# Merged instruction streams in a hybrid diffusion step: a recorder that counts changes between whole and part-array products

## The chip, the cores and the metric

The kernel runs on one core of a Trainium2 chip. The metric is the device time of one execution in microseconds; lower is better. The engines of the core work side by side, each through its own instructions in the order in which the program was written: TensorE (PE in the profile, its weight loads PEld), VectorE (DVE), ScalarE (ACT), GpSimd (POOL), and SyncE (SP), which issues the DMAs. They wait for each other by semaphores.

## The reference

One step of a two-layer backbone in f32. There are 128 prompt tokens and 1024 sample tokens, 1152 together, of width 1024. Each layer does the following (cut to what matters):

```python
h = rms_norm(x, g) * (1 + scale) + shift          # scale, shift, gate from the condition
parts = split_columns(h @ w_in)                   # one projection, 8384 columns
o_a = mla_attention(...) * silu(gate_a)           # latent attention, 8 heads, 1152 keys
o_b = b_in * short_conv(c_in * x_in, w) * silu(gate_b)
o_c = gdn_branch(...)                             # gated DeltaNet, both directions
m = s_a * (o_a @ w_pa) + s_b * (o_b @ w_pb) + s_c * (o_c @ w_pc)   # s_* = sigmoid(merge_g)
x = x + gate * (m @ w_o)
```

The DeltaNet works in chunks of 64 tokens with 8 heads of 64 x 64. In every chunk a triangular system is solved, and the chunks of a head are chained by their state:

```python
def step(state, xs):
    u_i, w_i, qd_i, kd_i, at_i, gl_i = xs
    v_new = u_i - einsum('bhck,bhkv->bhcv', w_i, state)
    o_i = einsum('bhck,bhkv->bhcv', qd_i, state) + einsum('bhij,bhjv->bhiv', at_i, v_new)
    state = state * exp(gl_i)[..., None, None] + einsum('bhck,bhcv->bhkv', kd_i, v_new)
    return state, o_i
```

## The kernel before

**Stages.** `start` loads and computes the modulation and the first normalised tokens. Then each layer goes through `front` (line 795: projection, convolutions, DeltaNet, and then the expansion of the latents), `attention` (written out by hand, without the recorder) and `mix` (line 1955: gates, branch projections, output projection, the next layer's norm, and the first tiles of the next layer's projection).

**Whole products.** The token axis is cut in three pieces of 384. Activations and weights of the projections are split into a high and a low part of f32r, and one tile of 128 x 128 weights makes three products of 128 rows, 128 columns and 384 tokens: `ip` in the projection (8 row blocks, so 24 products for a tile and a piece of tokens; 38 column tiles in `front`, four more in the attention), `mg`, `pp`, `wop` in `mix`, `ukp`, `uvp`, `uqp` for the latents. They use the whole array.

**Part-array products.** The DeltaNet's products are f32 and small, and each uses a part of the array, so that several can lie beside each other. An f32 product shows as two matmuls in the trace. `s_ga` (line 1540) makes the decay (`sg`, a whole product) and the chunk products `G` (64 x 64, 128 columns), `s_gb` solves the 32 x 32 triangles on VectorE and GpSimd without TensorE, `s_gz` (line 1715) joins them with 16 products of 32 x 32 (`pw`) from `P`, ScalarE's copy `ws`, and 16 more, then four copies by ScalarE. `s_gc` (line 1762) is the recurrence: for each of 16 steps and each of four pairs of heads, four products `p` (state by key), a scaling on VectorE and two adds of `vT` into the two halves of `scr`, four products `pv` whose inputs are these halves, a scaling, four products `pk`, and two updates of the state `SH` on VectorE, one for each direction. A fifth job does the prompt in two steps, four chunks at once. `s_gd` (line 1868) makes the outputs: `oi` (query by state) and `oa`. The four or more products of one phase alternate the direction, so that the second product needs the second half of what VectorE makes.

**The order of the work.** All of this is written as generators ("streams"). While one runs, `Eng` (line 82) does not issue an instruction but records it as an `Op` with its engine, what it reads and writes, and a cost in us (`cost`, line 115). `Flow.run` (line 228) merges the streams: it looks at the first open instruction of each, works out when it could start by its own clock (`ready`, line 159, from costs and a table of lags between engines; and `free`, when the engine is done), takes the best, and `put` (line 189) advances the clock and issues the instruction for good. So the order on every engine is fixed when the program is built, by the costs that the recorder believes. The choice weighs the time with a rank:

```python
best = min(cand, key=lambda x: (x[0] + 0.02 * x[1], x[1]))
...
    WIN = 0.3
    PREF = 0.5
...
RK = dict(ad=1, mk=0, mkb=5, xl=0, adl=1, w=2, ip=9, ev=1, cv=4, la=0, ga=7, gb=6, gv=4, gz=4, gc=3, gd=4, w2=2, lb=3, ln=0, ln1=1,
```

A smaller rank goes first. The projection `ip` has rank 9, the last of all: it fills the time in which the DeltaNet's streams (`ga` to `gd`, ranks 3 to 7) are not ready. A stream of better rank that will be ready a little later than the chosen one is waited for (`WIN`, `PREF`). `front` first runs the merged streams until the DeltaNet is done, and then goes on with what is left of `ip` beside the latents' streams (`lb`, `ln`).

**The prices before.** An f32r product costs `n / 2400` us from 256 columns on, an f32 one `4 n / 2400`. A product with at most 64 weight rows costs its weight columns over 1200 (over 600 where its output begins at partition 0). A change between whole and part-array products costs nothing.

Of the kernel before, what the change touches and what calls it, by code (L numbers as in the profile page):

```python
# [39 lines left out]


class Op:
    __slots__ = ("e", "f", "r", "w", "c", "m")


class Wait:
# [35 lines left out]
class Eng:  # L82
# [7 lines left out]
    def __getattr__(self, m):  # L90
        real = getattr(self.real, m)

        def call(*a, **kw):
            if not self.k.rec:
                return real(*a, **kw)  # L95
            op = Op()
            op.e = self.e
            op.f = lambda: real(*a, **kw)  # L98
            aps = [x for x in a if hasattr(x, "tensor")]
            out = kw.get("out")  # L100
            outs = [out] if out is not None else [aps.pop(0)]
            if kw.get("accum_out") is not None:
                outs.append(kw["accum_out"])
            ins = aps + [v for n, v in kw.items() if n not in ("out", "accum_out") and hasattr(v, "tensor")]
            if m == "matmul" and not kw.get("start", True):
                ins.append(outs[0])
            op.w = [(self.k.key(x), _span(x)) for x in outs]
            op.r = [(self.k.key(x), _span(x)) for x in ins]
            op.c = self.cost(m, outs[0], ins, kw)
            op.m = ins[0].ap[-1][1] / 1200.0 if self.e == "PE" else 0.0  # L110
            return op

        return call

    def cost(self, m, out, ins, kw):
        n = max([_free(out)] + [_free(x) for x in ins if x.space != DRAM]) if self.e != "PE" else _free(out)
        if self.e == "PE":
            if m == "transpose":
                return n * 2 / 2400.0
            r = ins[1].dtype == F32R  # L120
            t = n * ((1 if n >= 256 else 4) if r else 4) / 2400.0
            if ins[0].ap[0][1] <= 64:
                t = ins[0].ap[-1][1] / (1200.0 if out.offset // out.ap[0][0] else 600.0)
            return t
# [9 lines left out]
        for x in [out] + ins:  # L134
            c = 1
# [8 lines left out]
class Flow:  # L144
# [8 lines left out]
    def __init__(self, k):  # L153
        self.k = k
        self.free = {}
        self.log = {}
        self.ev = set()

    def ready(self, op):
        t = 0.0  # L160
# [28 lines left out]
    def put(self, op, s):  # L189
        f = self.free  # L190
        if op.e == "SP":
            f["SP"] = s + 0.06
            hw = max(s, f.get("HW", 0.0))
            f["HW"] = hw + 0.45
            d = max(hw + 1.1, f.get("DMA", 0.0))
            f["DMA"] = d + op.c
            self.note(op, d + op.c)
        else:
            if op.e == "PE":
                s = max(s, f.get("PEW", 0.0) + op.m)  # L200
                f["PEW"] = s
            f[op.e] = s + op.c
            self.note(op, s + op.c)
        op.f()
# [23 lines left out]
    def run(self, streams, until=None, evs=()):  # L228
# [5 lines left out]
        while True:  # L234
# [8 lines left out]
            cand = []  # L243
            for n in names:
                op = streams[n]["head"]
                if op is not None:
                    cand.append((max(self.free.get(op.e, 0.0), self.ready(op)), streams[n]["rank"], n, op))
            if not cand:
                raise RuntimeError("streams wait for each other: %s" % {n: streams[n]["wait"] for n in names})
            best = min(cand, key=lambda x: (x[0] + 0.02 * x[1], x[1]))  # L250
            for x in cand:
                if x[3].e == best[3].e and x[1] < best[1]:
                    wait = x[0] - best[0]
                    if wait <= 0 or wait < self.WIN and wait < self.PREF * (best[3].c - wait):
                        best = x
                        break
            streams[best[2]]["head"] = None
            self.put(best[3], best[0])

    WIN = 0.3  # L260
    PREF = 0.5


RK = dict(ad=1, mk=0, mkb=5, xl=0, adl=1, w=2, ip=9, ev=1, cv=4, la=0, ga=7, gb=6, gv=4, gz=4, gc=3, gd=4, w2=2, lb=3, ln=0, ln1=1,
# [2053 lines left out]
```

## Time and profile before

| | |
|---|---|
| median of 3 runs | 3682.22 us (3678.1 to 3687.41) |
| the profiled execution | 3702.81 us, its span 3701.0 us |
| PE busy | 3543.0 us (96%), 24330 matmuls |
| PEld busy | 3080.1 us (83%) |
| DVE busy | 1969.5 us (53%) |
| POOL busy | 1396.8 us (38%) |
| ACT busy | 1102.2 us (30%) |
| DMA | 336.79 MB, 91 GB/s over the span |
| mean granted TensorE clock | 0.957 of full speed |
| largest matmul groups | `ip` x5328, 1167.0 us, mean 358 ns; `mg` x3456, 623.2 us, mean 335 ns; `pp` x1728, 329.2 us, mean 341 ns |

The span runs from the first to the last instruction. Matmuls are pipelined: a single one is shown with its whole passage through the array, so that the shown duration (358 ns) is longer than the distance to the next one. Distances between the starts of rows in the timeline tell more than durations. In the timeline equal neighbours are merged into one row with their number; an idle time before a row stands in brackets with what ended it.

### The profile page before, as it was taken

Reading aid. Unit: us, or ns where it says so; the run is one execution under the profiler, and the core shown is the slowest. Engines: PE = TensorE matmul, PEld = TensorE weight load, DVE = VectorE, ACT = ScalarE, POOL = GpSimd, SP = SyncE. Lnnn points to the kernel's source line nnn. Section 1 sums busy time; section 2 is a strip of 40 time slices with the busy share of each in tenths; the row PEclk is TensorE's granted clock in tenths of the full one; section 3 lists DMA queues with packets and bytes.
Section 4 is the critical chain, followed back from the end, with each engine's and each line's share of the span. In section 5 each row is a group of like instructions: output and inputs, shape, how many; then the busy total and the mean of one; then the engine's idle time right before and its main releaser. Section 6 shows DMA issues by size and latency. Waiting matters only on the chain. (4 is left out here: it accounts for less than half of the span.)

```text
span 3701.0 us, 62464 instructions
## 1 busy us (share of the span) xinstructions
PE 3543.0 (96%) x24330; PEld 3080.1 (83%) x24330; DVE 1969.5 (53%) x4492; ACT 1102.2 (30%) x2327; POOL 1396.8 (38%) x1456
## 2 busy tenths in 40 slices
PE   7999999998999999999999999999999999999998
PEld 4988777777876789999999877777887667999998
DVE  4477676755555234541575777776455542131236
ACT  4432222224233222221344232212242332121234
POOL 3165555432266401332122645653323662123311
PEclk8999899999998899999999989999999998999999
DMA  5332212225622133441233222311364222132222
GB/s 184 93 106 74 57 54 72 68 59 171 185 66 67 47 111 113 121 127 52 101 101 95 87 75 79 77 48 55 98 223 117 69 61 67 56 95 61 81 79 88
DMA packets 315207, 336.79 MB, mean 91 GB/s; under 512 B 146208, under 2 KB 231904, under 8 KB 314528
## 3 DMA queue, kind: packets, MB, share of 16 engines
q1 hardware_dynamic: 314912, 332.80, 30.6%
q8 instruction: 192, 3.15, 0.3%
q14 instruction: 103, 0.84, 0.1%
HBM read 240.16 MB, written 92.47 MB: 90 GB/s over the span
## 5 line engine op out<-in xcount | busy, mean ns | idle before, releaser
L98 PE MATMUL ip<-h,wh_wi 128*128 128x384 f32 x5328 | 1167.0, 358 | 2.3 <-DVE gb L98 1.1
L98 PEld LDWEIGHTS ip<-h,wh_wi 128*128 128x128 f32 x5328 | 933.0, 194 | 54.4 <-issue 15.9
L98 PE MATMUL mg<-h,wh_mg 128*128 128x384 f32 x3456 | 623.2, 335 | 2.5 <-ACT mt L98 2.5
L98 PEld LDWEIGHTS mg<-h,wh_mg 128*128 128x128 f32 x3456 | 602.0, 188 | 3.1 <-ACT mt L98 3.1
L95 POOL TENSOR_TENSOR acc<-acc,P 128x512 f32<-128x512 f32 x224 | 290.2, 1295 | 199.7 <-ACT P L95 188.0
L95 DVE TENSOR_REDUCE mx<-s 128x1 f32<-128x384 f32 (+1 forms) x400 | 206.8, 540 | 240.4 <-PE s L95 239.3
L98 PE MATMUL pp<-ob,wp 128*128 128x384 f32 x1728 | 329.2, 341 | 2.3 <-DVE mU L98 1.2
L98 POOL TENSOR_TENSOR tmp<-M,X 128x2 f32<-128x2 f32 (+30 forms) x310 | 217.7, 702 | 277.1 <-DVE X L98 258.2
L98 PEld LDWEIGHTS pp<-ob,wp 128*128 128x128 f32 x1728 | 305.9, 191 | 11.1 <-DVE mt L98 6.6
L95 PE MATMUL st<-q,K 97*128 97x512 f32 (+1 forms) x912 | 290.4, 434 | 0.0
L95 ACT ACTIVATE P<-st 128x512 f32<-128x512 f32 x292 | 174.5, 598 | 351.4 <-PE st L95 314.7
L98 POOL TENSOR_TENSOR wh_mg<-wrm,wh_mg 128x512 fp32r<-128x512 f32 x88 | 117.1, 1333 | 424.0 <-ACT wh_mg L98 353.5
L98 POOL TENSOR_TENSOR mU<-mU,mt 128x384 f32<-128x384 f32 x96 | 108.3, 1128 | 327.2 <-DVE mt L98 327.1
L95 PEld LDWEIGHTS st<-q,K 97*128 97x128 f32 x912 | 185.1, 215 | 42.7 <-issue 24.3
L98 POOL TENSOR_TENSOR wh_wi<-wri,wh_wi 128x512 fp32r<-128x512 f32 x112 | 153.4, 1380 | 160.0 <-ACT wh_wi L98 157.9
L98 PE MATMUL wop<-mh,wh_wo 128*128 128x384 f32 x1152 | 203.6, 336 | 3.4 <-DVE mt L98 3.4
L98 PEld LDWEIGHTS wop<-mh,wh_wo 128*128 128x128 f32 x1152 | 199.8, 188 | 5.1 <-DVE mt L98 4.0
L98 DVE TENSOR_REDUCE X<-tmp 128x1 f32<-128x2 f32 (+30 forms) x620 | 184.5, 319 | 31.3 <-POOL tmp L98 23.4
L98 DVE SCALAR_TENSOR_TENSOR mt<-mt,pp 128x384 f32<-128x384 f32 x96 | 53.1, 553 | 254.5 <-ACT mt L98 239.9
L98 ACT ACTIVATE VT<-pv,sst 128x64 f32<-128x64 f32 x256 | 66.7, 311 | 367.0 <-DVE scr L98 350.7
L98 DVE TENSOR_TENSOR tmp<-M,X 128x2 f32<-128x2 f32 (+30 forms) x310 | 163.0, 526 | 20.9 <-POOL M L98 15.0
L98 ACT ACTIVATE mt<-mg 128x384 f32<-128x384 f32 x144 | 70.3, 488 | 339.9 <-PE mg L98 329.7
(302 smaller groups left out, 5104.5 us busy)
## 6 DMA issues: line engine op xcount, KB each, us to landing
wri<-in_w_in SPq DMA_DIRECT2D x160, 256.0 KB, 3.4
wrm<-in_w_in SPq DMA_DIRECT2D x96, 256.0 KB, 3.0
wada<-in_w_ada SPq DMA_DIRECT2D x64, 256.0 KB, 3.0
or<-oD SPq DMA_DIRECT2D x72, 192.0 KB, 3.0
wrp<-in_w_p SPq DMA_DIRECT2D x48, 256.0 KB, 3.0
gD<-gt SPq DMA_DIRECT2D x48, 192.0 KB, 1.9
KNd<-hl_uk SPq DMA_DIRECT2D x24, 384.0 KB, 3.4
QNd<-hl_uq SPq DMA_DIRECT2D x24, 384.0 KB, 3.7
```

The costliest lines, as they stand in the source:

```text
L95: return real(*a, **kw)
L98: op.f = lambda: real(*a, **kw)
```

## The change

The recorder learns of two kinds of products: `q` is true where the weights have at most 64 rows or at most 64 columns. It remembers the kind that PE did last (`part`). In `put`, a PE instruction of the other kind starts `SW` = 0.095 us after PE is free. In the choice, a part-array product whose turn would be a change counts as ready `HOLD` = 0.2 us later, and a whole product after a part-array one can start `STAY` = 0.1 us after PE is free at the earliest. The start that `put` uses is worked out again without these two. The prices of f32r and f32 products are new as well: 0.4514 ns a column, with a least price of 0.112 us for a pass, and two passes for f32. No instruction is added or removed; their order is what changes.

```diff
--- before.py
+++ after.py
@@ -40,7 +40,7 @@
 
 
 class Op:
-    __slots__ = ("e", "f", "r", "w", "c", "m")
+    __slots__ = ("e", "f", "r", "w", "c", "m", "q")
 
 
 class Wait:
@@ -108,6 +108,8 @@
             op.r = [(self.k.key(x), _span(x)) for x in ins]
             op.c = self.cost(m, outs[0], ins, kw)
             op.m = ins[0].ap[-1][1] / 1200.0 if self.e == "PE" else 0.0
+
+            op.q = self.e == "PE" and min(ins[0].ap[0][1], ins[0].ap[-1][1]) <= 64
             return op
 
         return call
@@ -118,7 +120,7 @@
             if m == "transpose":
                 return n * 2 / 2400.0
             r = ins[1].dtype == F32R
-            t = n * ((1 if n >= 256 else 4) if r else 4) / 2400.0
+            t = max(n * 0.4514e-3, 0.112) if r else 2 * max(n * 2 / 2400.0, 0.112)
             if ins[0].ap[0][1] <= 64:
                 t = ins[0].ap[-1][1] / (1200.0 if out.offset // out.ap[0][0] else 600.0)
             return t
@@ -155,6 +157,7 @@
         self.free = {}
         self.log = {}
         self.ev = set()
+        self.part = False
 
     def ready(self, op):
         t = 0.0
@@ -197,8 +200,9 @@
             self.note(op, d + op.c)
         else:
             if op.e == "PE":
-                s = max(s, f.get("PEW", 0.0) + op.m)
+                s = max(s, f.get("PEW", 0.0) + op.m, f.get("PE", 0.0) + (self.SW if op.q != self.part else 0.0))
                 f["PEW"] = s
+                self.part = op.q
             f[op.e] = s + op.c
             self.note(op, s + op.c)
         op.f()
@@ -244,7 +248,11 @@
             for n in names:
                 op = streams[n]["head"]
                 if op is not None:
-                    cand.append((max(self.free.get(op.e, 0.0), self.ready(op)), streams[n]["rank"], n, op))
+                    t = self.ready(op)
+                    if op.e == "PE" and op.q != self.part:
+
+                        t = max(t + self.HOLD, self.free.get("PE", 0.0)) if op.q else max(t, self.free.get("PE", 0.0) + self.STAY)
+                    cand.append((max(self.free.get(op.e, 0.0), t), streams[n]["rank"], n, op))
             if not cand:
                 raise RuntimeError("streams wait for each other: %s" % {n: streams[n]["wait"] for n in names})
             best = min(cand, key=lambda x: (x[0] + 0.02 * x[1], x[1]))
@@ -255,10 +263,14 @@
                         best = x
                         break
             streams[best[2]]["head"] = None
-            self.put(best[3], best[0])
+            self.put(best[3], max(self.free.get(best[3].e, 0.0), self.ready(best[3])))
 
     WIN = 0.3
     PREF = 0.5
+
+    SW = 0.095
+    HOLD = 0.2
+    STAY = 0.1
 
 
 RK = dict(ad=1, mk=0, mkb=5, xl=0, adl=1, w=2, ip=9, ev=1, cv=4, la=0, ga=7, gb=6, gv=4, gz=4, gc=3, gd=4, w2=2, lb=3, ln=0, ln1=1,
```

## Rows read from the trace of the kernel before

**Rows 1.** Busy time by stretch: reference stretch, the two mixed stages; columns in first line.
```profile
core 0: us, PE busy (x) PEld busy (x) DVE busy (x) ACT busy (x) POOL busy (x), PEclk, DMA share, GB/s
210.00:860.00 650.00, 617.24 (x6125) 498.23 (x6125) 452.48 (x1292) 170.41 (x457) 340.69 (x416) 0.94 0.26 72
...
2000.00:2660.00 660.00, 630.43 (x6280) 513.09 (x6280) 459.53 (x1304) 174.93 (x468) 344.65 (x431) 0.96 0.26 71
...
3200.00:3500.00 300.00, 299.85 (x1712) 296.20 (x1712) 70.64 (x111) 62.30 (x119) 78.34 (x66) 1.00 0.25 76
```

**Rows 2.** Timeline of PE, 355 to 363 us: start, us, engine, line, operation, shape, number.
```profile
355.20 1.68 PE L98 MATMUL ip<-h,wh_wi 128*128 128x384 f32 x8
356.96 0.67 PE L98 MATMUL pv<-scr,ZT 64*64 64x64 f32 x8
...
357.56 0.96 PE L98 MATMUL ip<-h,wh_wi 128*128 128x384 f32 x4
358.45 0.34 PE L98 MATMUL pk<-scr,kt 64*64 64x64 f32 x8
358.73 0.79 PE L98 MATMUL ip<-h,wh_wi 128*128 128x384 f32 x3
359.49 0.29 PE L98 MATMUL p<-SH,kTb 64*64 64x64 f32 x2
359.71 0.44 PE L98 MATMUL ip<-h,wh_wi 128*128 128x384 f32 x1
360.08 0.34 PE L98 MATMUL p<-SH,kTb 64*64 64x64 f32 x6
360.35 1.34 PE L98 MATMUL ip<-h,wh_wi 128*128 128x384 f32 x6
361.62 0.32 PE L98 MATMUL pv<-scr,ZT 64*64 64x64 f32 x2
361.88 0.44 PE L98 MATMUL ip<-h,wh_wi 128*128 128x384 f32 x1
362.25 0.44 PE L98 MATMUL pv<-scr,ZT 64*64 64x64 f32 x6
362.62 0.62 PE L98 MATMUL ip<-h,wh_wi 128*128 128x384 f32 x2
```

**Rows 3.** Waits of PE, 210 to 860 us: us in total, times, longest us.
```profile
PE pv L98 <- DVE scr L98: 7.6, 14, 1.4
```

**Rows 4.** Timeline of PE near 326 us, one row of its pattern.
```profile
325.96 0.25 PE L98 MATMUL pw<-ZT,P 32*32 32x32 f32 x4 [0.19 <-ACT ZT L98]
```

**Rows 5.** Groups of VectorE, 210 to 860 us: busy us, mean ns, idle before.
```profile
L98 DVE TENSOR_TENSOR scr<-scr,vT 64x128 f32<-64x128 f32 x128 | 54.0, 422 | 3.6
```

**Rows 6.** Timeline of PE near 2459 us, two streams in one run.
```profile
2458.07 0.79 PE L98 MATMUL ip<-h,wh_wi 128*128 128x384 f32 x3
2458.82 0.34 PE L98 MATMUL p<-SH,kTb 64*64 64x64 f32 x8
2458.96 0.63 PE L98 MATMUL oi<-SH,qTb 64*64 64x128 f32 x8
2459.52 0.96 PE L98 MATMUL ip<-h,wh_wi 128*128 128x384 f32 x4
```

**Rows 7.** Timeline of PE near 247 and near 2386 us.
```profile
247.18 1.09 PE L98 MATMUL G<-kqT 64*64 64x128 f32 x16
248.20 2.00 PE L98 MATMUL ip<-h,wh_wi 128*128 128x384 f32 x10
...
2386.12 1.09 PE L98 MATMUL G<-kqT 64*64 64x128 f32 x16
2387.14 0.45 PE L98 MATMUL pw<-ZT,ws 32*32 32x32 f32 x32
```

**Rows 8.** Stretches behind the mixed stages, instructions on `ip` alone.
```profile
860.00:960.00 100.00, 22.72 (x112) 19.45 (x112) 3.29 (x6) 2.44 (x5) 0.97 0.60 204
...
2660.00:2790.00 130.00, 45.76 (x236) 40.46 (x234) 5.92 (x11) 4.87 (x10) 0.99 0.67 217
```

## The prediction

> **What bounds the kernel now.** Read first the table by stretches. In the reference stretch of pure whole-array work, 1712 products take 300 us, so one whole product costs the array 0.175 us, at the full clock [rows 1]. The two stretches in which the DeltaNet streams run beside the projection (I call them the mixed stages: 210 to 860 us for layer 0, 2000 to 2660 us for layer 1) have PE "busy" for 617 of 650 and 630 of 660 us [rows 1]. Next to that VectorE has 452 and 460, GpSimd 341 and 345. So PE sets the pace there, but its busy time hides what this change is about: the busy time of a matmul includes the pipeline, and a row looks busy while the array changes over.
>
> The timeline of PE shows it. A whole product that follows another starts 0.175 us later; every part-array run costs far more than its own work. I price a run as the time from the start of the row of `ip` before it to the start of the `ip` row after it, less 0.175 us for each product of the first row. A `p` run of 2 matmuls (one f32 product is two of the trace's matmuls) costs 359.71 - 358.73 - 3 x 0.175 = 0.46 us; the `p` run of 6 behind it 360.35 - 359.71 - 0.175 = 0.47 us; a `pk` run of 8 358.73 - 357.56 - 4 x 0.175 = 0.47 us [rows 2]. So two, six or eight cost the same: it is the change of the array that is paid, on the way in and out, and not the products. With `pv`: 2 matmuls 0.48 us, 6 matmuls 0.57 us [rows 2]. In the two mixed stages I count 652 part-array runs, one in every 2.0 us; at about 0.46 us each, some 300 of 1310 us go into them.
>
> The waits are small: the largest one of PE in layer 0's mixed stage, `pv` for VectorE's `scr`, adds up to 7.6 us [rows 3]. PE arrives late at its part runs, not early.
>
> **The change, part by part.**
>
> *Split runs.* The products of one group often come ready in two steps, because VectorE makes their inputs in two halves. The old recorder then puts one `ip` product into the gap: `p` 2, `ip` 1, `p` 6, and `pv` 2, `ip` 1, `pv` 6 [rows 2]; `pw` 4, `ip` 1, `pw` 28, whose first row is [rows 4]. I count 50, 25 and 30 such triples over both stages. Under the new rules the run starts a little later (the hold), and once it has begun, `ip` stands back by 0.1 us and pays 0.095 us, so the second half follows directly.
> - `p`: 0.46 + 0.47 becomes 0.47, a gain of 0.46 us at best. If the joined run waits for its second half as the `pv` row below does (0.38 us), 0.08 is left. VectorE's second half is a short update and the hold covers most of it, so I take 0.46: 25 x 0.46 = 12 us (bounds 2 to 12).
> - `pv`: apart they cost 0.48 + 0.57 = 1.05. Joined, without waiting, not less than the 0.57 of the six, so the gain is at most 0.48. A run of 8 that stands joined now costs 357.56 - 355.20 - 8 x 0.175 = 0.96 us [rows 2], since it begins with the first half and waits 0.38 us for the other: gain 0.09. VectorE's add between the halves takes 422 ns [rows 5], and the recorder believes 0.065 + 128/960 = 0.198. The hold moves the start by about 0.2 us, so I take the middle, 0.28: 50 x 0.28 = 14 us (bounds 4 to 24).
> - `pw`: its first four matmuls wait for ScalarE's copies [rows 4], and the rest for two more. I bound the gain by the rows of `p` and `pv`, 0.08 to 0.48, and take 0.3 for the longer second wait: 30 x 0.3 = 9 us (bounds 2 to 14).
>
> Sum 35 us (bounds 8 to 50).
>
> *Joined streams.* Of 652 runs 547 remain, one per 2.4 us. The hold delays a part product by 0.08 to 0.25 us (0.2 less the lead that its rank gives it over `ip`, plus what is left of a whole product), and standing back adds up to 0.1. A window of 0.25 to 0.3 us in 2.4 catches a neighbour in about one run of nine: 60 joins. What one saves: `p` 8 and `oi` 8 together cost 2459.52 - 2458.07 - 3 x 0.175 = 0.92 us [rows 6], so `oi` adds 0.45 behind `p`. Alone I estimate it from the entry, 360.08 - 359.71 - 0.175 = 0.195 [rows 2], and half of the 1.02 us that sixteen products of its shape take [rows 7]: 0.70, hence 0.25 saved. The bounds are 0 and the 0.46 of the `p` pair. Not every neighbour is of the same tiling. From the first of sixteen 64 x 64 matmuls of `G` to the next row it is 1.02 us when a whole product follows and 1.02 us when a 32 x 32 `pw` follows [rows 7]: going to another small tiling costs the exit in full. I count a quarter of the joins as such and at nothing: 45 x 0.25 = 11 us (bounds 0 to 120 x 0.25 = 30).
>
> [...]
>
> *Lost cover.* The old recorder underprices PE: a whole product at 384/2400 = 0.160 us, a run of four products at 2 x 0.107 + 2 x 0.053 = 0.32 with the change-over free, against 0.175 and 0.47. With some six products between runs that is 6 x 0.015 + 0.15 = 0.24 us per run by which PE now comes later than planned, and that covers VectorE, which is slower than planned as well [rows 5]. The new prices take this cover away and the hold gives about 0.2 back. What is missing, 0.05 us x 547 runs = 27 us, is felt where the input is the last to come, say half: +14 us. Bounds: the hold more than covers, and the present waits shrink (-10), or it gives nothing, 0.24 x 547 / 2 = +65. Behind a waiting part product stand, in PE's order, the `ip` products whose evictions feed the convolutions, and ScalarE's copies of `pv`.
>
> *Edits with one answer.* The new prices of short whole products, the flag on the 2- and 4-row products of the conditioning, and DMA issues that the recorder orders anew in all streams: nothing, since the attention's order is written by hand and does not pass the recorder, the stretch from 3200 to 3500 us is full whatever the order, and the DMA engines are busy for 0.26 of the mixed stages [rows 1]. A few us either way. SP's and POOL's queues get the same instructions.
>
> Sum: -35 - 11 + 14 = -32 us. The profiled execution took 3702.8 us, 0.6% above the median of 3682.2; the difference is taken off the median: **3650 us**.
>
> **Rivals.**
> 1. *Full gain.* The joined runs wait for nothing and the cover suffices: -50 - 60 x 0.25 - 10 = -75, 3607 us. For: PE comes late at present, and its largest wait is 1% of the stage [rows 3]. Against: the joined `pv` that waits 0.38 us [rows 2].
> 2. *Given back in waits.* The cover term reaches some 45 us, and the time is 3682 as before. For: VectorE's 422 ns against 198 planned [rows 5], and 70% busy [rows 1]. [...] The flag may change little, since 0.12 of the 0.2 us is eaten by the ranks. [...]
> 3. *Slower: the held chain.* The recurrence has 194 part-array steps per layer, one behind the other. If these and not PE set the end of the stage, 0.2 us of hold at each makes it 39 us longer. The filler decides: after the DeltaNet ends, 112 `ip` matmuls are left in layer 0 (20 us at 0.175) and 236 in layer 1 (41 us) [rows 8]. What goes beyond is time. The price lies between 39 - 20 = 19 us, and 78 us if the phase behind, with its DMA engines busy for 0.60 and 0.67 [rows 8], cannot become shorter at all: about 45 us, 3727 us. For: the recorder will believe in less room than before. Against: PE waits little now, so the chain has slack.
>
> **How the numbers follow.** About 0.3% (11 us) is what a measurement of this kernel can tell from no change. Forecast 0.46, its own range 3625 to 3671; full gain 0.19; given back 0.21; held chain 0.14. Faster: forecast and full gain, 0.65; same 0.21; slower 0.14. The range of 8 in 10 goes from 3595, below the full gain, to 3700, which takes in the given-back case and the cheap end of the held chain; most of the dear end and the last of the joins at their bounds (50 + 30 + 10) stay outside.
>
> **What would show it.** In the profile after: triples of 2, `ip` 1 and 6 nearly gone from the timeline; some 490 part runs in place of 652; `pv` 8 the usual form, at 0.6 to 0.96 us; PE's waits for `scr` and `SH` up, but by less than 30 us; both mixed stages shorter or with more `ip` left behind them. The forecast is wrong if the runs stay above 600 (the change doesn't do it), if the waits eat the joins (rival 2), or if the stage behind the DeltaNet runs out of `ip` (rival 3).

## The result and the profile after

The changed kernel is **slower**: 3727.19 us median (3722.82 to 3735.8), ratio to the kernel before 1.0106, 95% interval 1.007 to 1.0141. The forecast was 3650 us, in a range of 3595 to 3700. All ratios below are against runs of the kernel before on the same chip at the same time; here these are four, 3678.1 to 3712.23 us.

The page of the changed kernel, its first lines:

```profile
span 3727.0 us, 62487 instructions
...
PE 3512.5 (94%) x24330; PEld 3081.7 (83%) x24330; DVE 1969.6 (53%) x4492; ACT 1103.0 (30%) x2327; POOL 1375.1 (37%) x1456
```

PE is busy 30.5 us less than before (3543.0), and the span is 26 us longer: the joins did take work away, and idle time took more back. The same by stage; the first fence is the kernel before, the second the one after. Each has `front` of layer 0 (from the first `ip` product to the first of the attention), `front` of layer 1, and then the two stages of `mix` (from the first `mg` product to the next layer's first `ip`, and to the end).

```profile
54.90:961.40 906.50, 853.87 (x7463) 721.20 (x7464) 594.22 (x1558) 279.15 (x684) 403.05 (x488) 0.95 0.30 90
1903.40:2775.50 872.10, 835.60 (x7462) 709.82 (x7461) 578.36 (x1535) 268.05 (x662) 378.94 (x471) 0.97 0.32 94
...
1313.70:1903.43 589.73, 580.52 (x3314) 573.71 (x3313) 272.89 (x427) 164.77 (x296) 127.98 (x110) 0.99 0.33 103
3126.19:3701.03 574.84, 559.30 (x3193) 551.92 (x3192) 181.68 (x289) 155.25 (x280) 124.12 (x104) 0.99 0.25 78
```

```profile
58.40:952.80 894.40, 824.49 (x7462) 714.10 (x7463) 588.71 (x1558) 279.48 (x684) 391.48 (x488) 0.95 0.31 91
1915.40:2793.60 878.20, 820.22 (x7461) 712.28 (x7461) 577.38 (x1536) 269.53 (x662) 379.50 (x471) 0.95 0.32 94
...
1306.54:1915.41 608.87, 590.17 (x3314) 578.98 (x3313) 273.14 (x427) 164.31 (x296) 120.17 (x110) 0.98 0.32 100
3141.61:3726.98 585.37, 563.23 (x3193) 553.37 (x3192) 186.54 (x289) 154.68 (x280) 121.40 (x104) 0.99 0.24 77
```

Columns as in [rows 1]. The second column less PE's busy time is PE's idle time. In the two fronts PE's busy time falls by 29.4 and 15.4 us, and its idle time grows by 17.3 and 21.5 (69.9 and 58.0 after, 52.6 and 36.5 before). The attention stages stay (352.3 and 350.7 us before, 353.7 and 348.0 after). What makes the kernel slower is `mix`, +19.1 and +10.5 us, and there are no part-array products there at all.

The waits of PE over the whole trace of after; before, the first three were 17.0, 11.5 and 10.5 us:

```profile
PE pv L98 <- DVE scr L98: 36.0, 58, 2.4
PE sg L98 <- POOL gm L98: 22.2, 23, 3.4
PE p L98 <- DVE SH L98: 21.1, 51, 2.5
...
PE pp L98 <- DVE mt L98: 7.7, 21, 1.5
...
PE adc L98 <- DVE ada L98: 7.0, 8, 1.9
```

In the mixed stages the change does what it says. The timeline of PE after, in the same stretch of the recurrence as [rows 2]:

```profile
350.56 0.47 PE L98 MATMUL pv<-scr,ZT 64*64 64x64 f32 x8
350.97 1.16 PE L98 MATMUL ip<-h,wh_wi 128*128 128x384 f32 x5
352.05 0.34 PE L98 MATMUL pk<-scr,kt 64*64 64x64 f32 x8
352.33 0.97 PE L98 MATMUL ip<-h,wh_wi 128*128 128x384 f32 x4
353.23 0.34 PE L98 MATMUL p<-SH,kTb 64*64 64x64 f32 x8
353.50 1.49 PE L98 MATMUL ip<-h,wh_wi 128*128 128x384 f32 x7
355.32 0.67 PE L98 MATMUL pv<-scr,ZT 64*64 64x64 f32 x8 [0.33 <-DVE scr L98]
...
359.69 0.69 PE L98 MATMUL ip<-h,wh_wi 128*128 128x384 f32 x3
360.31 0.38 PE L98 MATMUL pv<-scr,ZT 64*64 64x64 f32 x5
360.48 0.32 PE L98 MATMUL G<-kqT 64*64 64x128 f32 x1
360.48 0.28 PE L98 MATMUL pv<-scr,ZT 64*64 64x64 f32 x3
360.59 1.03 PE L98 MATMUL G<-kqT 64*64 64x128 f32 x15
361.55 0.44 PE L98 MATMUL ip<-h,wh_wi 128*128 128x384 f32 x1
```

Runs of 8 without a gap are the rule. `pv` now waits for `scr` ahead of its run (0.33 us at 355.32). At 360.31 two streams share a run: `pv` 8 and `G` 16 (24 of the trace's matmuls) take 361.55 - 359.69 - 3 x 0.175 = 1.34 us; in the kernel before, `G` 16 takes 1.02 us from its first row to the next [rows 7] and `pv` 6 takes 0.57 with its entry [rows 2], together 1.59 and `G`'s entry besides. The triples of the old order are gone: runs of one product kind parted by a single whole product went from 54, 28 and 23 (`pv`, `p`, `pw`) to none. Part-array runs went from 700 to 537 in the whole trace, and from 655 to 492 in the two fronts.

The DeltaNet ends sooner (layer 0 at 800.4 us instead of 846.9, layer 1 at 2618.5 instead of 2657.4), but that is only the projection put off. The windows behind it, on `ip` alone, as in [rows 8]:

```profile
800.40:952.80 152.40, 90.10 (x474) 82.60 (x474) 7.77 (x15) 8.78 (x18) 1.00 0.55 183
2618.50:2793.60 175.10, 116.00 (x613) 106.80 (x613) 7.82 (x15) 11.74 (x24) 1.00 0.53 176
```

474 and 613 `ip` products are left there. Counted from the last `ot`, the last product of the DeltaNet, the kernel before had 176 and 249.

### The profile page after: what moved, and what is told of

Same layout as the page of the kernel before. It is cut to its first block, busy times and chain, and to the rows that moved or that the text cites. A ratio compares the mean times of both kernels' runs of the same rounds, so it can differ in the third digit from the quotient of the medians.

```text
span 3727.0 us, 62487 instructions
## 1 busy us (share of the span) xinstructions
PE 3512.5 (94%) x24330; PEld 3081.7 (83%) x24330; DVE 1969.6 (53%) x4492; ACT 1103.0 (30%) x2327; POOL 1375.1 (37%) x1456
## 4 chain that ended last, share of the span: by engine, by line
PE 64%; DVE 16%; DMA 8%; POOL 5%; issue 4%; ACT 2%; SPq 1%; DVEq 0%; ACTq 0%; POOLq 0%
PE ip L98 16%; PE mg L98 10%; PE pp L98 6%; PE st L95 6%; PE wop L98 5%; PE po L95 4%; DMA wada<-in_w_ada 4%; DVE scr L98 3%; PE fg L95 3%; PE s L95 2%; DVE X L98 2%; DVE tmp L98 2%; DVE ada L98 2%; PE sm L95 2%; POOL tmp L98 2%
## 5 line engine op out<-in xcount | busy, mean ns | idle before, releaser
L98 PE MATMUL ip<-h,wh_wi 128*128 128x384 f32 x5328 | 1138.8, 356 | 0.0
L98 PEld LDWEIGHTS ip<-h,wh_wi 128*128 128x128 f32 x5328 | 940.6, 195 | 40.6 <-issue 13.5
L98 PE MATMUL pp<-ob,wp 128*128 128x384 f32 x1728 | 331.0, 341 | 13.7 <-DVE mt L98 7.7
L98 POOL TENSOR_TENSOR tmp<-M,X 128x2 f32<-128x2 f32 (+30 forms) x310 | 226.4, 730 | 253.7 <-DVE X L98 247.4
L98 DVE TENSOR_REDUCE X<-tmp 128x1 f32<-128x2 f32 (+30 forms) x620 | 186.8, 319 | 35.7 <-POOL tmp L98 27.3
```

## The experiments

One table for all runs: median ratio to before with its interval, the length of four stages in the profiled execution (us), and the `ip` products left behind the DeltaNet in layers 0 and 1.

| kernel | ratio | front 0 | mix 0 | front 1 | mix 1 | left |
|---|---|---|---|---|---|---|
| before | 1 | 906.5 | 589.7 | 872.1 | 574.8 | 176, 249 |
| after | 1.0106 [1.007, 1.0141] | 894.4 | 608.9 | 878.2 | 585.4 | 474, 613 |
| e1_prices_only | 1.0174 [1.0148, 1.02] | 908.2 | 613.1 | 882.1 | 584.9 | 354, 498 |
| e2_rules_only | 0.9922 [0.9896, 0.9948] | 879.9 | 583.7 | 856.0 | 574.6 | 205, 324 |
| e3_mix_old_prices | 0.9999 [0.9982, 1.0016] | 895.6 | 587.2 | 878.0 | 574.3 | 474, 613 |
| e4_no_hold | 1.0175 [1.0153, 1.0196] | 910.9 | 613.5 | 898.9 | 584.3 | 471, 615 |
| e5_f32_price_only | 0.9999 [0.998, 1.0018] | 884.1 | 587.4 | 873.4 | 575.0 | 181, 396 |
| e6_longer_lag | 1.0085 [1.0057, 1.0114] | 887.8 | 603.3 | 883.7 | 583.7 | 295, 367 |
| e7_cheaper_price | 0.9965 [0.9946, 0.9984] | 891.2 | 580.6 | 865.8 | 573.4 | 24, 176 |
| e8_rules_hold_35 | 0.9936 [0.9913, 0.9959] | 891.1 | 582.8 | 861.7 | 575.3 | 103, 252 |
| e9_all_prices_exact | 1.0146 [1.0117, 1.0175] | 923.0 | 595.2 | 890.3 | 577.3 | 0, 0 |
| e10_old_pe_exact_rest | 1.0176 [1.0147, 1.0205] | 934.3 | 578.2 | 904.2 | 572.9 | 0, 0 |
| e11_front_f32r_only | 1.0008 [0.9987, 1.0029] | 887.4 | 583.5 | 884.5 | 574.3 | 429, 615 |
| e12_kq_price | 0.9977 [0.9957, 0.9997] | 892.1 | 587.8 | 872.3 | 573.8 | 181, 396 |
| e13_mix_exact_rest | 0.9941 [0.9919, 0.9963] | 891.6 | 578.2 | 862.7 | 574.4 | 205, 324 |
| e14_mix_pe_act_exact | 1.007 [1.0045, 1.0094] | 898.0 | 612.8 | 859.8 | 584.2 | 205, 324 |
| e15_f32r_167 | 1.0015 [0.9994, 1.0037] | 888.4 | 587.0 | 880.7 | 574.9 | 322, 438 |
| e16_f32r_153 | 0.9929 [0.9903, 0.9954] | 885.0 | 586.3 | 856.5 | 573.8 | 111, 186 |
| e17_front_153_mix_exact | 0.9856 [0.982, 0.9892] | 877.0 | 576.8 | 860.0 | 572.9 | 111, 186 |
| e18_mix_pe_dve_exact | 0.9994 [0.9962, 1.0026] | 890.8 | 593.6 | 861.1 | 583.2 | 205, 324 |

What a single stage length can tell: e2, e13, e14 and e18 issue the same instructions to PE in the same order in front 0, and its length there is 879.9 to 898.0 us. So the ratios decide, and a stage only where the difference is larger.

### The change taken apart: prices, rules, hold

e1 is the kernel before with the new price line alone; e2 is the changed kernel with the old one, the same two lines the other way round:

```diff
-            t = n * ((1 if n >= 256 else 4) if r else 4) / 2400.0
+            t = max(n * 0.4514e-3, 0.112) if r else 2 * max(n * 2 / 2400.0, 0.112)
```

> Edit: the recorder of before with the new prices of whole products alone; no kinds, no hold, no standing back. Lost-cover theory (the exact prices take away the slack by which PE used to come later than planned, and that slack covered VectorE): slower than before, since nothing is gained against it: mix 15 to 30 us longer as after, waits of PE for scr, SH and gm up as after (36, 21 and 22 us there), part runs still about 650, and the time 3715 to 3760. Rival, the hold and the standing back themselves cost what is lost: prices alone change nothing, 3675 to 3695.

> Edit: the changed kernel with the old prices of whole products; SW, HOLD and STAY stay. Lost-cover theory: the joins come without the loss, part runs about 500, mix as before (590 and 558 us from the first gate product to the last output product), the time 3630 to 3665, faster than before. Rival, the rules themselves cost: as slow as the change, 3710 to 3730, with waits for scr above 30 us.

The rules bring 0.8% alone (0.9922) and 0.7% on top of the new prices (1.0174 to 1.0106). The prices cost 1.7% alone, and 1.8% on top of the rules. The two parts add, and the change is slower for its prices, not for its rules.

By their ratios both times came out as the theory of the lost cover expected, but e1's waits did not. Those of PE for `scr` and `SH` were to rise to 36 and 21 us under the prices alone. Here they are for before, e1 and e2:

```profile
PE pv L98 <- DVE scr L98: 17.0, 37, 1.4
PE p L98 <- DVE SH L98: 10.5, 22, 1.4
...
PE pv L98 <- DVE scr L98: 18.0, 46, 1.4
PE p L98 <- DVE SH L98: 14.8, 34, 1.6
...
PE pv L98 <- DVE scr L98: 28.6, 57, 2.6
PE p L98 <- DVE SH L98: 24.7, 47, 1.7
```

The sums are 27.5, 32.8 and 53.3 us, and 57.1 after. So it is the rules that bring most of these waits, and the new prices add 4 to 5 us.

e4 is the changed kernel without the hold. e8 is e2 with a longer one (`+    HOLD = 0.35`).

```diff
-    HOLD = 0.2
+    HOLD = 0.0
```

> Edit: the changed kernel with HOLD = 0; SW, STAY and the new prices stay. If the hold was what still covered VectorE (lost-cover theory), the waits for scr and SH grow beyond 36 and 21 us and the time rises to 3735 to 3770, with some 30 part runs more. If the held chain costs (rival 3 of the prediction), the time falls by 20 us or more, to below 3710.

> Edit: the rules with the old prices, and HOLD = 0.35 in place of 0.2. The hold is cover too (without it the change lost another 28 us): lost-cover theory 3640 to 3665, with part runs below 480 in the mixed stages and the waits for scr below 25 us. Rival (the held chain): the recurrence gets longer by 194 x 0.15 = 29 us a layer, the filler runs out, 3680 to 3720.

Without the hold, the rest of the rules brings nothing (1.0175, as e1), although part-array runs in the fronts fall from e1's 659 to 516. So the gain needs the hold, and fewer runs are not yet a gain; the hold without `SW` and `STAY` was not tried. The waits, which were to grow, stay at 37.1 and 19.3 us. More hold gives no more (0.9936 beside 0.9922, overlapping), with 483 runs and a wait for `scr` of 26.1 us, just above what was expected.

### Where the prices cost: mix

e3 is the changed kernel with the old price line wherever the stage is `mix` (a flag that is set there), so `front` keeps the new one.

```diff
+            if self.k.mixing:
+                t = n * ((1 if n >= 256 else 4) if r else 4) / 2400.0
```

> Edit: the changed kernel, but streams recorded in mix are priced as before; front keeps the new prices. Lost-cover theory: mix goes back by about 20 us in layer 0 and 10 us in layer 1, so 3685 to 3705, and what is then still lost against the joins is in front. Rival (mix is slower because front hands it another order of DMAs and buffers, and not by the prices): within 5 us of the changed kernel, 3720 to 3735.

1.0106 to 0.9999: the new prices cost 1.07%, 39 us, in `mix` alone, although every product there is a whole one and the new price, 0.173, is the right one (4.16 us for 24 products, below; the old price is 0.160). The stages show 33 us of it, 608.9 and 585.4 against 587.2 and 574.3.

How a right price costs time is seen, for a part of it, at one step. The branch product `pp` waits for VectorE's product `mt`, and that for ScalarE's tanh of the gate tile `mg`. To hide this chain, the order puts gate products of the next tile ahead of `pp`. All engines but PEld, first before, then after:

```profile
3314.79 4.33 PE L98 MATMUL mg<-h,wh_mg 128*128 128x384 f32 x24
3317.47 0.63 ACT L98 ACTIVATE wh_mg<-wrm 128x512 fp32r<-128x512 f32 x1 [5.74 <-PE mg L98]
3318.00 0.47 ACT L98 ACTIVATE mt<-mg 128x384 f32<-128x384 f32 x1
...
3318.51 0.55 DVE L98 SCALAR_TENSOR_TENSOR mt<-mt,pp 128x384 f32<-128x384 f32 x1 [6.19 <-ACT mt L98]
3319.12 2.38 PE L98 MATMUL pp<-ob,wp 128*128 128x384 f32 x12
```

```profile
3332.70 4.32 PE L98 MATMUL mg<-h,wh_mg 128*128 128x384 f32 x24
3335.55 0.63 ACT L98 ACTIVATE wh_mg<-wrm 128x512 fp32r<-128x512 f32 x1 [5.74 <-PE mg L98]
3336.08 0.47 ACT L98 ACTIVATE mt<-mg 128x384 f32<-128x384 f32 x1
...
3336.59 0.56 DVE L98 SCALAR_TENSOR_TENSOR mt<-mt,pp 128x384 f32<-128x384 f32 x1 [6.19 <-ACT mt L98]
3337.20 2.35 PE L98 MATMUL pp<-ob,wp 128*128 128x384 f32 x12 [0.18 <-DVE mt L98]
```

In both, ScalarE first splits a weight tile (`wh_mg`, released by an `mg` product), then does the tanh, and from the start of the split to `pp` it is 1.65 us. What differs is how many products PE has in that time: 24 `mg` products take 4.16 us, so in the kernel before PE is free at 3314.79 + 4.16 = 3318.95, 0.17 us ahead of `pp`, and after at 3332.70 + 4.16 = 3336.86, 0.34 us ahead. I counted over the whole stage: before, 51 of 61 such steps of layer 1 have ten gate products of the next tile ahead of `pp`; after, 57 of 64 have nine. The chain that the recorder believes in is about 1.5 us, which is ten products at 0.160 (9 x 0.160 = 1.44 is too few) and nine at 0.173 (1.56). The old price was wrong by 8% and so left one product of slack for an engine whose price is wrong by more: the tanh takes 487 ns and is believed to take 0.13 + 384/1600 = 0.37 us. Of the 64 steps of layer 1 after, 44 cost nothing beyond 0.173 us and one 0.1 us. All else, 8.2 us, lies in 19 steps, in each of which the tanh stands right behind a split on ScalarE. The kernel before loses 2.6 us in 15 such steps.

Fourteen of the 19 steps are that one product: 0.34 us in place of 0.17. But 3.4 us lie in three others (1.30, 0.86 and 1.19 us). In two of these the split that holds up the tanh itself waits for VectorE, and in the third there are two splits ahead of it; the kernel before has no step of layer 1 above 0.31 us. One of the two:

```profile
3284.09 0.53 ACT L98 ACTIVATE ob<-or 128x384 fp32r<-128x384 f32 x1 [2.45 <-DVE or L98]
3284.53 0.47 ACT L98 ACTIVATE mt<-mg 128x384 f32<-128x384 f32 x1
```

In all three fences the tanh starts 0.09 or 0.10 us before the shown end of the split ahead of it: here 0.44 us after the start of a split of 0.53 us, above 0.53 us after the start of one of 0.63.

Beyond 0.173 us for each product, the step is 5.8 us of mix 1's 10.5; 2.0 more lie between `wop` products, 1.8 between `pp` products and 0.8 where `wop` begins. Of mix 0's 19.1 the step is 5.5; 2.9 and 2.0 are the steps from `mg` and `pp` to the condition's products `adc`, and `mg` products in a row take 5.8 us more, which goes with 27.3 us at the lower level of the granted clock (0.50 of full speed in the trace) in place of 13.7.

If the slack is the cause, other slack should cure it. e6 adds 0.2 us to the recorder's lags from ScalarE, VectorE and GpSimd to PE; e9 gives those three engines prices nearer to the measured ones; e10 does the same with PE at the old prices. The first change of the diff is e6's, the rest e9's:

```diff
-    ... ("ACT", "PE"): 0.28 ... ("DVE", "PE"): 0.26 ... ("POOL", "PE"): 0.22
+    ... ("ACT", "PE"): 0.48 ... ("DVE", "PE"): 0.46 ... ("POOL", "PE"): 0.42
-            return (0.131 if m == "scalar_tensor_tensor" else 0.065) + n / ...
+            return (0.2 if m == "scalar_tensor_tensor" else 0.15) + n / ...
-            return (0.307 if ... else 0.13) + n / 1600.0
+            return (0.307 if ... else 0.245) + n / 1600.0
-            return (0.15 if m != "tensor_tensor" else 0.1) + n / (1200.0 if m != "tensor_tensor" else 475.0)
+            return (0.15 if m != "tensor_tensor" else 0.2) + n / (1200.0 if m != "tensor_tensor" else 450.0)
```

> Edit: the changed kernel with its exact prices, but the recorder's lags from ScalarE, VectorE and GpSimd to PE are 0.2 us longer each. The lost-cover theory says that any allowance does: the waits for scr, SH and gm fall below 25, 15 and 15 us, mix comes back by 15 us or more in layer 0, and the time is 3640 to 3690. Rival (the old prices lead to another mixture of gate and branch products or another order of loads, and cover has nothing to do with it): 3710 to 3740, as changed.

> Edit: the changed kernel with its exact PE prices, and the prices of the other engines raised to what the trace shows: ScalarE from PSUM 0.245 + n/1600 us (384 elements: 0.49 measured, 0.37 before), VectorE 0.15 or 0.2 + n/960 (128 elements 0.286 against 0.198), GpSimd 0.2 + n/450 (512 elements 1.33 against 1.18). If the change lost because PE alone was priced exactly while the engines that it waits for stayed too cheap, the step from gate to branch products in mix loses its 0.1 us (mix 582 to 592 and 574 to 578 us), and the time is 3640 to 3680. Rival (exact prices of PE hurt by themselves, by another mixture of the streams): mix stays at 600 and 583 or more, 3710 to 3750.

> Edit: the rules, PE priced as before (too cheap), the other engines priced exactly. If cover is worth more than the old prices gave, the waits of PE for scr, SH and gm fall below 20, 15 and 12 us and the time is 3630 to 3660, below the rules alone. If the old mispricing of both sides was already in balance, 3655 to 3685; too much cover shows as in the run with cheaper f32r products (waits of the latents' norms behind the DeltaNet up, 3670 or more).

The longer lag gives ten products again, but only some of the time back (603.3 and 583.7; 5.3 us beyond 0.173 at the step in layer 1): the tanh still stands behind the splits. As a whole e6 missed what the theory expected and lies at its rival's (1.0085). Prices nearer to the measured ones for all engines give most of it (595.2 and 577.3), and with the old PE price more than all (578.2 and 572.9). Yet as a whole e9 and e10 are 1.5 and 1.8% slower than before, by their fronts, which are told below; both times missed the gain that was expected. (VectorE's new price is near for its short products from PSUM, 0.283 against 0.287 us; the add of `vT` into `scr`, 0.467 us after, stays too cheap.)

e13, e14 and e18 have the rules, the old prices in `front`, and in `mix`: the old PE price with e9's for the other three (e13); the new PE price with e9's for ScalarE (e14); the new PE price with e9's for VectorE (e18).

```diff
+            if self.k.mixing:
+                return (0.2 if m == "scalar_tensor_tensor" else 0.15) + n / 960.0
```

The lines are VectorE's in e13 and e18; ScalarE's and GpSimd's in `mix` are e9's numbers under the same condition.

> Edit: the rules; front as in the rules-only kernel; in mix PE is priced as before (too cheap) and ScalarE, VectorE and GpSimd exactly. In the run with old PE prices and the rest exact, mix took 578 and 573 us against 584 and 575 for the rules alone, and the front lost; taken together this should give 5 to 8 us below the rules alone: ratio 0.987 to 0.993. If the gain in mix goes with that run's front, 0.993 or more.

> Edit: the rules; front with old prices; in mix the exact PE prices of the change, and of the other engines only ScalarE's price from PSUM raised from 0.13 to 0.245 + n/1600 us. If the loss in mix is the step gate product, tanh on ScalarE, multiply on VectorE, branch product, whose planned 1.51 us fall short of the measured 1.65, the recorder now plans 1.63 us, ten products instead of nine, and mix is at 583 to 592 and 574 to 578 us, the ratio 0.992 to 0.997. If VectorE's or GpSimd's price or the short products matter as much, mix stays at 598 and 580 or more, the ratio 1.000 to 1.006.

> Rules kept, front at the old prices, in mix the new TensorE prices and of the other engines VectorE's alone as measured (0.15 or 0.2 us + n/960). If it is VectorE's slack that the new TensorE price takes from the step from gate product to branch product, the stages of mix fall back from 609 and 585 us to some 585 and 577, the excess at mg to pp from 9 to below 4 us, ratio 0.993 to 0.998. If GpSimd's price is what did it in the run with all prices exact, they stay near 610 and 584, the excess above 6 us, ratio 1.001 to 1.007.

e13 puts eleven products there (51 of 60 steps), and the step costs nothing any more, split or not. Its mix 0 is 5.5 us shorter than e2's, but its ratio, 0.9941, is no better than e2's 0.9922 (they overlap) and missed the 0.987 to 0.993 expected. ScalarE's price alone cures nothing: 612.8 and 584.2. It does put ten products there (59 of 65 steps of layer 1), as was planned, and the step still costs 7.0 us, 4.7 of them in five steps of 0.23 to 1.44 us. So nine products in place of ten are only a part of what the price does; which order ScalarE's and VectorE's work gets is another, and was not tried by itself. VectorE's cures mix 0 (593.6, as e9) and not mix 1 (583.2), so e18's ratio came out between the two cases that were written down: 0.7% slower than e2, where e14 is 1.5%. For mix 1 neither suffices. Whether GpSimd's alone does, or only all three, was not tried.

### Where the prices cost: front

e3 still holds the new prices in `front`, and lies 0.77% (28 us) above e2. e5 and e12 divide them: e5 has the old f32r price in all stages and the new f32 one, e12 of the new prices only that of the 128 x 2 products `kq` (0.224 us; the old recorder believed 0.003, the trace shows two matmuls of 0.112 us from start to start). e11 has the new f32r price and the old f32 one, in `front` alone.

```diff
-            t = max(n * 0.4514e-3, 0.112) if r else 2 * max(n * 2 / 2400.0, 0.112)
+            t = n * (1 if n >= 256 else 4) / 2400.0 if r else 2 * max(n * 2 / 2400.0, 0.112)
...
+            if not r and n == 2:
+                t = 0.224
...
+            t = max(n * 0.4514e-3, 0.112) if r else n * 4 / 2400.0
```

(e5, e12 and e11, in this order; in e12 all other products have the old price, and e11's line holds in `front`.)

> Edit: the rules as changed, the new price for f32 products alone; f32r is priced as before (0.160 us for 384 columns). If the cover lies in the price of the many f32r products (15600 of the 24330 matmuls are f32r of 384 columns), this stays near the rules alone: 3655 to 3685. If it is the f32 price, above all of the 128 conditioning products in mix of layer 0 and the row sums, most of the loss comes back: 3700 to 3730, with mix of layer 0 at 600 us or more.

> Edit: the rules with the old prices, and the new price (0.224 us) only for f32 products of 2 columns, which are the row sums of the keys and queries (144 in the two layers). If these are the f32 price's cost in front (under the old prices the recorder took the 32 of a job for nothing, so that PE came about 7 us later than planned at each), the ratio is 0.997 to 1.003, as with the f32 price everywhere. If it is the other f32 products (row sums of the norms, decays), 0.989 to 0.996.

> Edit: the rules; in front (and start) f32r is priced exactly and f32 as before, in mix all as before. By the runs so far the front's loss of 0.77% is the f32 price and the mix's of 1.07% the f32r price, so this should stand at the rules alone: ratio 0.988 to 0.997. If f32r in front costs as well, 0.998 to 1.005.

The f32 prices alone cost 0.77% beside e2 (e5, between its two cases, with mix 0 at 587.4 us), `kq` alone 0.55%, f32r alone 0.86%, all together 0.77%. Each price that is made right costs about the same, and they don't add. e11 missed what was expected of it.

A dose of the f32r price asks whether each order is a draw of its own. With the rules, and `mix` and f32 at the old prices, one product in `front` costs 0.153 (e16), 0.160 (e2), 0.167 (e15) or 0.173 us (e11). e7 has 0.144 in all stages. The lines of e16:

```diff
+            if r and n >= 256 and not self.k.mixing:
+                t = n * 0.4e-3
```

> Edit: the rules as changed, the old prices, and f32r products from 256 columns on another tenth cheaper (0.144 us for 384 columns, where the trace has 0.173). If more cover is still worth something, 3635 to 3660, below the rules alone (ratio 0.992), with PE's waits for scr under 25 us. If 0.160 covers enough, the same within 10 us; if too much cover starves the streams in the end, 3670 or more with over 20 us of idle PE behind the DeltaNet.

> Edit: the rules with the old prices, but f32r in front at 0.167 us for 384 columns (0.160 gave ratio 0.992, 0.173 gave 1.001). Smooth theory (cover falls as the price rises): between, 0.994 to 0.999, with 250 to 430 and 380 to 620 ip matmuls left behind the DeltaNet. Draw theory (each order is its own): anything from 0.988 to 1.004, not between.

> Edit: as the one before, with f32r in front at 0.153 us. Smooth theory: between 0.160 (0.992) and 0.144 (0.9965, in both stages): 0.991 to 0.997, with fewer ip matmuls left behind the DeltaNet (60 to 200 and 200 to 320) than at 0.160. Draw theory: not between, below 0.989 or above 0.999.

In the order of the prices 0.9965, 0.9929, 0.9922, 1.0015, 1.0008: the same at 0.153 and 0.160, a step of 0.9% up to 0.167, the same at 0.173. With the dearer product fewer of them are put between the DeltaNet's: 111 and 205 are left behind it in layer 0 at 0.153 and 0.160, 322 and 429 at 0.167 and 0.173, so PE reaches the DeltaNet's products earlier. At 0.144 only 24 are left, and by its time e7 is the third of its cases, too much cover. e16 is where the smooth theory had it (but for 186 products left in layer 1, not 200 to 320), and e15 lies outside that theory's range, so five orders don't settle it.

What the clock makes of it can be estimated. Over 94 executions of the kernel before, on five chips, the time goes with the mean granted clock, from 3662 us at 0.967 to 3711 at 0.955: a straight line gives 2.9 us for each thousandth. By this line, set to the clock of the kernel before on their chip, the five are 38, 31, 23, 3 and 8 us below it. By this estimate the loss at 0.144 goes with its clock, and the step between 0.160 and 0.167 does not.

The other end is in e9 and e10. With full slack the DeltaNet lasts so long that no `ip` is left behind it, and the norms of the latents, which it would hide, are waited for. e9's waits of PE, then its two fronts:

```profile
PE pv L98 <- DVE scr L98: 21.6, 37, 1.8
PE rs_kv L98 <- DVE ssakv L98: 21.5, 4, 8.5
PE rs_cq L98 <- DVE ssacq L98: 13.2, 4, 4.2
```

```profile
52.10:975.10 923.00, 838.46 (x7463) 723.11 (x7464) 594.43 (x1559) 278.70 (x684) 398.03 (x489) 0.91 0.30 88
1920.20:2810.50 890.30, 824.65 (x7460) 709.81 (x7459) 582.51 (x1535) 267.63 (x662) 378.14 (x471) 0.94 0.31 92
```

`pv` waits 21.6 us, less than after's 36.0, but the `rs` products of the norms wait 34.7 us, and the granted clock of front 0 falls to 0.91. Over all their executions e9 and e10 have 0.944 and 0.933, where the kernel before has 0.961; by the line above that goes with 51 and 82 us, of the order of all that they lose (56 and 68). So too much slack costs where the filler runs out, by waits and with a lower clock. What too little costs in the fronts is not PE's waits for `scr` and `SH`: these are 53.3 us in e2, 47.2 in e15 and 56.3 in e11.

### Together

e17 joins e16's front and e13's mix.

> Rules kept; f32r products of the front at 0.153 us, f32 at the old price; in mix TensorE at the old prices and the other engines at the measured ones. If gains of the front (0.9929 with 0.153 alone) and of mix (0.9941 with measured prices of the other engines alone, beside 0.9922 of the rules alone) were separate terms that add, neither term is a gain over the rules alone: ratio 0.991 to 0.995. Rival (the cheaper front gives a gain that the layer behind takes up): below 0.990.

0.9856, the fastest of all and faster than both kernels of the change, and more than was expected: it fell on the rival's side, whose reason (that the layer behind takes up the gain) is not shown. The stages show a part of the gain: mix 0 is 9.5 us shorter than e16's, mix 1 0.9 us, which is 0.28% and would make 0.990. The rest, 0.4%, is within the two intervals (e16's reaches down to 0.9903, and that less 0.28% is 0.9875; e17's reaches up to 0.9892).

```profile
1278.80:1855.60 576.80, 572.84 (x3314) 569.55 (x3313) 275.44 (x422) 163.98 (x292) 127.53 (x110) 1.00 0.34 106
...
3066.60:3639.40 572.80, 556.62 (x3193) 551.85 (x3191) 187.70 (x289) 154.33 (x280) 123.44 (x104) 0.99 0.25 79
```

In mix 0 of e17 PE idles 4.0 us, where after it is 18.7.

## Why the prediction was wrong

**The step that failed is "Edits with one answer", in which the new prices were costed at "nothing".** Its reason, that "the stretch from 3200 to 3500 us is full whatever the order", took a property of the order before for one of the stage. With the old price that stretch has ten products where the chain needs 1.65 us; with nine the wait in each step behind a split doubles, and other steps get new waits. The term was 39 us (after against e3; 33 in the stages, of which 11 are this step) and stood at zero, with the price line quoted in the change. It was noted of the mixed stages that an underpriced PE is cover, and `mix` was left out of that thought. In the prediction's terms the rules alone gave -29 us (-46 was forecast), the new prices +28 in the fronts (+14) and +39 in `mix` (0): together +38, where 39 was measured.

**The lost cover was under-sized, and its waits came from the rules.** It was put at +14 us, with bounds of -10 and +65. The new prices cost 28 us in the fronts (e3 against e2), which lies within the bounds. PE's waits for `scr` and `SH` double, 27.5 to 57.1 us (up by less than 30 us was forecast, and 29.6 came), but 25.8 of that is there in e2, which has the joined runs and the price of the change-over (`SW`) and not the new prices. So that the 28 us are lost cover in the recurrence is not shown. The hold was said to give most of the cover back, and `kq`, whose price went from 0.003 to 0.224 us for 144 products, was not seen as cover at all: alone it is 0.55%.

**The joins were right in number.** 162 part-array runs fewer were forecast for the mixed stages, 163 came; the triples are gone; joined streams and split runs were put at 46 us together. PE's busy time in the two fronts fell by 44.8 us after. With the rules alone, as a mean of e2, e13, e14 and e18, it fell by 31.5 + 25.9 = 57 us, idle time rose by 29, and the fronts became 29 us shorter, which is also what e2's ratio gives (0.78% of 3682). Without the lost cover the forecast comes to -46 us. A joined `pv` was forecast to take 0.6 to 0.96 us, waits included; its median is 0.98, just above. From the last product before a run to the first behind it, less 0.173 us, all part-array runs of the two fronts cost 455 us before, 433 in e2 and 448 after. And e4 has most of the joins without any gain.

**The rivals.** Full gain did not come. Rival 2 (given back in waits) is what happened in the fronts: they are 12.1 us shorter and 6.1 longer. The clock is a part too: its mean is 0.9525 in the four executions after and 0.9614 in the 94 before, which by the line above goes with some 26 us. Rival 3 had the right sign and, by luck, the right number, 3727, by another way. The recurrence with the hold ran shorter, and the filler did not run out: 474 and 613 products were left. A filler that runs out was seen in e9 and e10, where the slack is much larger.

What stays open: by what the new prices cost 28 us in the fronts, why the step there lies between 0.160 and 0.167 us, and which of the other engines' prices frees mix 1. Of the 28 us in the fronts, the traces (means of e2, e13, e14, e18 against after and e3) show 23, 18 of them in layer 1: 13.5 are PE busy longer and 9.7 idle. The clock's mean falls from 0.9616 in e2 to 0.9558 in e3, which by the line above goes with 17 us; whether the order lowers the clock was not tried.

## What to carry to other kernels

A scheduler's wrong price can be the slack that another wrong price needs, so a price that is corrected to the measured value is not yet a gain. Here it was none alone (e1, 1.0174) nor together with the other engines' (e9, 1.0146), which helped one stage and cost in the other. Try each price by the time, stage by stage, and look at every stage that the same table plans, also at those without the thing that is changed. A stage whose bounding engine is full in the profile is full in that order; before an edit that reorders it is costed at nothing, find the chain that its products hide and count how many products it has to spare. Split such a change into its rules and its numbers first, since here the two parts were worth -0.8 and +1.8%.

## What was not expected of the hardware

**The same order has different clocks.** The granted clock has two levels in the traces, 0.50 and 1.00 of full speed (before: 0.50 from 385.3 to 416.0 us, 1.00 from there to 446.7). In front 0 of e2, e13, e14 and e18, with one order on PE, the time at the lower one was 56.1, 84.7, 108.0 and 88.3 us, and the stage took 879.9, 891.6, 898.0 and 890.8 us: about 0.35 us of stage for each us. The 94 executions of the kernel before give 0.38. Other orders have more or less of it in front 0 (157.5 us in e9, 68.1 in e17), but one execution doesn't tell such differences from its own scatter. The clock alone does not explain the change: by the line above some 13 of its 39 us stay at an equal clock, e1 is slower than after (1.0174) at a higher clock (0.9553), and with e3's prices `mix` is cured with fronts as long as after's.

**Two kinds of products of one tiling share a run for less than they cost apart.** `pv` and `G`, both 64 x 64, alternate at 360.48 us, and 24 matmuls of two streams take 1.34 us, where `G` 16 and `pv` 6 apart take 1.59 and `G`'s entry. Where `pw`, 32 x 32, follows `G`, the 1.02 us from `G`'s first row to the next are those in front of a whole product [rows 7].
